# Batched fp32 matmul on one Trainium2 core: the first input load cut into eight transfers, and the last store moved into the hand-written section

## The chip, the cores and the metric

The kernel runs on 1 core of one Trainium2 chip. The metric is device time in microseconds (us), here the median of 3 runs: 262.35 us before the change, with single runs from 262.20 to 262.47 us.

## The reference

```python
def setup_inputs():
    batch, m, k, n = 16, 512, 768, 1024
    return {
        "x": np.random.randn(batch, k, m).astype(np.float32),
        "y": np.random.randn(batch, k, n).astype(np.float32),
    }

def reference(x: np.ndarray, y: np.ndarray) -> np.ndarray:
    return np.einsum('bkm,bkn->bmn', x, y).astype(np.float32)
```

Sixteen independent products: for each batch the 768x512 x, transposed, times the 768x1024 y. The contraction index k leads both inputs, so x needs no transpose on the chip. Per batch 1.57 MB of x and 3.15 MB of y are read and 2.10 MB of output are written, all fp32.

## The kernel before

**Layout.** k is split as 128 partitions by 6 (`ko`), so that one partition of x holds 12 KB that lie together in memory (6 x 512 floats), one partition of y 24 KB, and one partition of the output 16 KB (4 rows of 1024 floats). A load or store of one batch is one DMA instruction over all 128 partitions.

**Buffers.** x and y land in fp32 in two buffers each (`xs`, `ys`, by the batch's parity). VectorE casts them to bf16 (`xb`, `yb`, two slots each; lines 124 and 128). TensorE multiplies: 48 matmuls with 512 columns per batch, in two groups of 24 that fill the two halves of PSUM (line 150, in a hardware loop over the batches). ScalarE copies each half to an fp32 output buffer (line 166); there are five of those (`ob`, `NO = 5`). SyncE (SP) issues all DMAs, loads and stores alike, in one order on one queue.

**Order of the queue.** The whole kernel is written by hand inside one section (`tile_critical`, lines 45 and 46), in which the programmer places all semaphore waits. SP's part is the loop at line 102: for batch b it issues x (line 106), y (line 109) and, from b = 4 on (`LAG`), the store of batch b - 4 (lines 93 to 100). From b = 2 on, x waits until VectorE has cast the x of two batches before, and y likewise. After the loop come the stores of batches 12, 13 and 14 (line 112). GpSimd (line 131) passes VectorE's progress on to TensorE.

**Two shapes of load.** `wide_dma` (line 69) issues the first transfer of each kind, x and y, as an ordinary DMA (line 73). Each later one is a copy of that instruction with another access pattern: four x partitions, or two y partitions, are read as one row of 48 KB.

**Semaphores of the loads.** Each transfer adds 16 to the semaphore of its buffer (`sx[i]`, `sy[i]`) when it is complete. VectorE waits for 16 times the number of transfers into that buffer so far (line 123).

**The end.** The last store, of batch 15, is not in the section. At lines 174 and 175 SP waits until the stores of batches 11, 12 and 13 have landed; at line 176 the section is closed, which makes all engines meet; and line 181 issues the store of batch 15 outside of it, so that the Tile framework sets the waits around it, and waits for it to land before the program ends (line 207, the end of the launch).

Of the kernel before, what the change touches and what calls it, by code (L numbers as in the profile page):

```python
# [1 line left out]

_os.environ.setdefault("NEURON_RT_ULTRASERVER_MODE", "4")

# [2 lines left out]

# [5 lines left out]


@with_exitstack
def kernel(
    ctx: ExitStack,
    tc: tile.TileContext,
    x: bass.AP,
    y: bass.AP,  # L20
    out: bass.AP,
):
    nc = tc.nc
    P = 128
    FP32 = mybir.dt.float32
    BF16 = mybir.dt.bfloat16

    B, K, M = x.shape
    _, _, N = y.shape
    KT = K // P  # L30
    MT = M // P
    NF = 512
    NT = N // NF

    x_v = x.rearrange("b (p ko) m -> b p ko m", ko=KT)
    y_v = y.rearrange("b (p ko) n -> b p ko n", ko=KT)
    o_v = out.rearrange("b (p mo) n -> b p mo n", mo=MT)

    LAG = 4
    NO = 5
    KH = KT // 2

    section = ExitStack()
    section.enter_context(tc.tile_critical())
    ec = ctx.enter_context
    xs = [ec(nc.sbuf_tensor(f"xs{i}", [P, KT, M], FP32)) for i in range(2)]
    ys = [ec(nc.sbuf_tensor(f"ys{i}", [P, KT, N], FP32)) for i in range(2)]
    xb = ec(nc.sbuf_tensor("xb", [P, 2, KT, M], BF16))  # L50
    yb = ec(nc.sbuf_tensor("yb", [P, 2, KT, N], BF16))
    ob = [ec(nc.sbuf_tensor(f"ob{i}", [P, MT, N], FP32)) for i in range(NO)]

    HB = MT // 2
    ps = [ec(nc.psum_tensor(f"ps{i}", [P, HB, NT, NF], FP32)) for i in range(2)]
    sx = [ec(nc.semaphore(f"sx{i}")) for i in range(2)]
    sy = [ec(nc.semaphore(f"sy{i}")) for i in range(2)]
    so = [ec(nc.semaphore(f"so{i}")) for i in range(NO)]
    cast = ec(nc.semaphore("cast"))
    ready = ec(nc.semaphore("ready"))  # L60
    room = ec(nc.semaphore("room"))
    groups = ec(nc.semaphore("groups"))
    idle = ec(nc.semaphore("idle"))
    outs = ec(nc.semaphore("outs"))


    made = {}

    def wide_dma(key, dst, src, dram_rows, load):


        if key not in made:
            made[key] = nc.sync.dma_start(dst, src)
            return made[key]
        pat = mybir.BassSymbolicTensorAccessPattern
        widen = lambda a: a.rearrange("(q r) k m -> q (r k m)", r=dram_rows)
        plain = lambda a: a.rearrange("p k m -> p (k m)")
        s, d = (widen(src), plain(dst)) if load else (plain(src), widen(dst))
        return nc.sync.add_instruction(_copy.replace(
            made[key].ins, name=nc.get_next_instruction_name(),  # L80
            ins=(pat(ap=s.ap, dtype=s.dtype, bass_ap=s, is_dma=False),),
            outs=(pat(ap=d.ap, dtype=d.dtype, bass_ap=d, is_dma=False),),
            sync_info=None, ant_dge_precooked=False))


    def parts(b):
        return 2 if b in (15,) else 1


    nx = [sum(1 + parts(a) for a in range(b)) + 1 for b in range(B)]  # L90


    def store(b):


        if b < B - 2:
            nc.sync.wait_ge(groups, 2 * (b + 2))
        else:
            nc.sync.wait_ge(outs, b - (B - 3))
        nc.sync.dma_start(o_v[b], ob[b % NO][:]).then_inc(so[b % NO], 16)  # L100

    for b in range(B):
        i = b % 2
        if b >= 2:
            nc.sync.wait_ge(cast, nx[b - 2])
        wide_dma("x", xs[i][:], x_v[b], 4, True).then_inc(sx[i], 16)
        if b >= 2:
            nc.sync.wait_ge(cast, nx[b - 2] + parts(b - 2))
        wide_dma("y", ys[i][:], y_v[b], 2, True).then_inc(sy[i], 16)
        if b >= LAG:  # L110
            store(b - LAG)
    for b in range(B - LAG, B - 1):
        store(b)


    for _ in range(60):
        nc.vector.sem_inc(idle, 1)
    for b in range(B):
        i = b % 2
        n = 16 * (b // 2 + 1)  # L120
        if b >= 2:
            nc.vector.wait_ge(groups, 2 * (b - 1))
        nc.vector.wait_ge(sx[i], n)
        nc.vector.tensor_copy(xb[:, i], xs[i][:]).then_inc(cast, 1)  # L124
        nc.vector.wait_ge(sy[i], n)
        for h in range(parts(b)):
            ks = slice(h * KT // parts(b), (h + 1) * KT // parts(b))
            nc.vector.tensor_copy(yb[:, i, ks], ys[i][:, ks]).then_inc(cast, 1)  # L128


    for b in range(B):
        nc.gpsimd.wait_ge(cast, nx[b]).then_inc(ready, 1)
        for h in range(parts(b)):
            nc.gpsimd.wait_ge(cast, nx[b] + h + 1).then_inc(ready, 2 // parts(b))


    x_w = xb[:].rearrange("p s k (j mo) -> p s k mo j", mo=MT)
    pe = OrderedEngineSet([nc.tensor.engine])
    with nc.Fori(0, B // 2, engines=pe):
        with nc.Fori(0, 2, engines=pe) as s:  # L140
            nc.tensor.wait_ge(ready, 2).then_inc(ready, -2)
            for mo in range(MT):
                g, m = divmod(mo, HB)
                if m == 0:
                    nc.tensor.wait_ge(room, 1).then_inc(room, -1)  # L145
                for kt in range(KT):
                    if mo == 0 and kt == KH:
                        nc.tensor.wait_ge(ready, 1).then_inc(ready, -1)
                    for nt in range(NT):
                        mm = nc.tensor.matmul(  # L150
                            ps[g][:, m, nt], x_w[:, bass.ds(s, 1), kt, mo],
                            yb[:, bass.ds(s, 1), kt, nt * NF:(nt + 1) * NF],
                            start=(kt == 0), stop=(kt == KT - 1))
                if m == HB - 1:
                    mm.then_inc(groups, 1)


    nc.scalar.nop().then_inc(room, 2)
    for _ in range(60):
        nc.scalar.sem_inc(idle, 1)  # L160
    for b in range(B):
        if b >= NO:
            nc.scalar.wait_ge(so[b % NO], 16 * (b // NO))
        for g in range(2):
            nc.scalar.wait_ge(groups, 2 * b + g + 1)
            cp = nc.scalar.copy(ob[b % NO][:, g * HB:(g + 1) * HB].rearrange("p m (t f) -> p m t f", f=NF),  # L166
                                ps[g][:])
            if b < B - 1:
                cp.then_inc(room, 1)
        if b == B - 2:  # L170
            nc.scalar.drain().then_inc(outs, 1)
    cp.then_inc(outs, 1)

    for b in range(B - LAG - 1, B - 2):
        nc.sync.wait_ge(so[b % NO], 16 * (b // NO + 1))
    section.close()

    nc.sync.dma_start(o_v[B - 1], ob[(B - 1) % NO][:])


# [1 line left out]
_INS = ['x', 'y']  # L185
_OUTS = [((16, 512, 1024), 'float32')]


# [23 lines left out]
```

## Time and profile before

| what | us |
|---|---|
| median of 3 runs | 262.35 |
| the profiled execution, its own time | 262.47 |
| its span, first to last instruction | 260.7 |
| around the span | 1.8 |
| PE busy (matmul) | 186.1 |
| VectorE busy | 82.0 |
| ScalarE busy | 61.1 |
| share of 16 DMA engines' span, queue q1 | 98.1% |

PE is TensorE's matmul row, DVE is VectorE, ACT is ScalarE, SPq is SP's instruction stream. A line number such as L150 is a line of the kernel. "DMA share" is the mean busy share of the 16 DMA engines; a packet is counted in the stretch in which it starts, with its whole duration, so that a short stretch can show more than 1. The granted TensorE clock is given as a share of full speed. "Waits" lists who waited for whom; the chain is the work that ended last, followed back. All times in the views count from the start of the span.

### The profile page before, as it was taken

How to read it: one execution, taken by the hardware profiler on the slowest of the kernel's cores; microseconds unless marked ns; L12 is line 12 of the kernel's file. 1: busy time of each engine (PE TensorE's matmuls, PEld its weight loads, DVE VectorE, ACT ScalarE, POOL GpSimd, SP SyncE). 2: the span in 40 equal slices, each digit the busy share in tenths (PEclk: the TensorE clock that was granted, in tenths of full speed). 3: DMA queues.
4: the chain of work that ended last, by engine and by line, in shares of the span. 5: the costliest groups of instructions: out<-in, count | busy, mean ns of one | idle time of the engine just before them, and what ended most of it. 6: DMA issues, size and time to landing. Idle time of an engine off the chain costs nothing. (4 is left out here: it accounts for less than half of the span.)

```text
span 260.7 us, 2506 instructions
## 1 busy us (share of the span) xinstructions
PE 186.1 (71%) x768; PEld 89.8 (34%) x768; DVE 82.0 (31%) x33; ACT 61.1 (23%) x33; POOL 0.2 (0%) x4
## 2 busy tenths in 40 slices
PE   0009999998937949479596894969959197696910
PEld 0004555554512515124242351434425043253500
DVE  0261644525222252312524115252142522225000
ACT  1000442243220222202214022040322205022220
POOL 0000000000000000000000000000000000000000
PEclk9999999999995999959889797797999889799985
DMA  7998999999899899989999989999998999999994
GB/s 260 432 494 385 468 385 468 392 392 488 385 410 493 370 450 475 427 385 405 483 400 437 465 367 453 410 483 402 410 485 382 445 468 417 410 410 430 427 410 181
DMA packets 4514, 109.07 MB, mean 418 GB/s; under 512 B 768, under 2 KB 768, under 8 KB 768
## 3 DMA queue, kind: packets, MB, share of 16 engines
q1 hardware_dynamic: 4512, 109.05, 98.1%
q14 instruction: 2, 0.02, 0.0%
HBM read 75.50 MB, written 33.55 MB: 418 GB/s over the span
## 5 line engine op out<-in xcount | busy, mean ns | idle before, releaser
L150 PE MATMUL ps<-yb,xb 128*128 x768 | 186.1, 407 | 62.7 <-PEq L145 60.7
L150 PEld LDWEIGHTS ps<-yb,xb 128*128 x768 | 89.8, 117 | 158.5 <-issue 92.2
L166 ACT COPY ob<-ps 128x2048 f32<-128x2048 f32 x32 | 59.8, 1870 | 184.2 <-PE ps L150 184.2
L128 DVE CAST yb<-ys 128x6144 bf16<-128x6144 f32 (+1 forms) x17 | 53.8, 3171 | 87.7 <-DMA ys<-in_y_dram 87.7
L124 DVE CAST xb<-xs 128x3072 bf16<-128x3072 f32 x16 | 28.2, 1760 | 69.4 <-DMA xs<-in_x_dram 65.3
L166 ACT ACT_TABLE_LOAD x1 | 1.3, 1283 | 5.3 <-issue 5.3
L196 POOL MEMSET const-bfloat16-1.0<- 128x1 bf16 x1 | 0.1, 102 | 0.0
L196 POOL MEMSET const-uint8-127<- 128x1 uint8 x1 | 0.1, 102 | 0.0
L196 POOL MEMSET const-float32-1.0<- 128x1 f32 x1 | 0.1, 99 | 0.0
L196 POOL MEMSET const-float32-0.0<- 128x1 f32 x1 | 0.1, 98 | 0.2 <-issue 0.2
## 6 DMA issues: line engine op xcount, KB each, us to landing
ys<-in_y_dram SPq DMA_DIRECT2D x16, 3072.0 KB, 28.2
out_dram<-ob SPq DMA_DIRECT2D x16, 2048.0 KB, 32.6
xs<-in_x_dram SPq DMA_DIRECT2D x16, 1536.0 KB, 29.7
```

The source lines that it names most:

```text
L124: nc.vector.tensor_copy(xb[:, i], xs[i][:]).then_inc(cast, 1)
L128: nc.vector.tensor_copy(yb[:, i, ks], ys[i][:, ks]).then_inc(cast, 1)
L150: mm = nc.tensor.matmul(ps[g][:, m, nt], x_w[:, bass.ds(s, 1), kt, mo], yb[:, bass.ds(s, 1), kt, nt * NF:(nt + 1) * NF], start=(kt == 0), ...
L166: cp = nc.scalar.copy(ob[b % NO][:, g * HB:(g + 1) * HB].rearrange("p m (t f) -> p m t f", f=NF), ps[g][:])
L196: nc = _bacc.Bacc("TRN2", target_bir_lowering=False, num_devices=1)
```

## The change

The first x (batch 0) is issued as eight DMA instructions ahead of the loop. Transfer c takes the 16 partitions c, c + 8, c + 16 and so on. All eight add 16 to `sx[0]`, so that VectorE's waits on that semaphore are raised by 7 x 16 = 112. `wide_dma("x")` is called from b = 1 on, so that the x of batch 1 is now the first of its kind, issued as an ordinary DMA.

At the end the section is no longer closed by hand. The store of batch 15 is issued by SP within the section like the others, behind a wait for ScalarE's last copy; then SP waits for all five store semaphores, that of batch 15's store first; then the section ends, and with it the kernel.

```diff
-    section = ExitStack()
-    section.enter_context(tc.tile_critical())
+    ctx.enter_context(tc.tile_critical())
...
+    x_first = x_v[0].rearrange("(a c) k m -> a c k m", c=8)
+    for c in range(8):
+        nc.sync.dma_start(xs[0][c::8], x_first[:, c]).then_inc(sx[0], 16)
     for b in range(B):
         i = b % 2
         if b >= 2:
             nc.sync.wait_ge(cast, nx[b - 2])
-        wide_dma("x", xs[i][:], x_v[b], 4, True).then_inc(sx[i], 16)
+        if b > 0:
+            wide_dma("x", xs[i][:], x_v[b], 4, True).then_inc(sx[i], 16)
...
-    for b in range(B - LAG, B - 1):
+    for b in range(B - LAG, B):
         store(b)
...
-        nc.vector.wait_ge(sx[i], n)
+        nc.vector.wait_ge(sx[i], n + (112 if i == 0 else 0))
...
-    for b in range(B - LAG - 1, B - 2):
-        nc.sync.wait_ge(so[b % NO], 16 * (b // NO + 1))
-    section.close()
-    nc.sync.dma_start(o_v[B - 1], ob[(B - 1) % NO][:])
+    for i in range(NO):
+        nc.sync.wait_ge(so[i], 16 * len(range(i, B, NO)))
```

## The prediction

> **What bounds the kernel now.** I read the page's DMA rows first: queue, rate by slice, issues.
>
> ```profile
> PE 186.1 (71%) x768; PEld 89.8 (34%) x768; DVE 82.0 (31%) x33; ACT 61.1 (23%) x33; POOL 0.2 (0%) x4
> DMA  7998999999899899989999989999998999999994
> q1 hardware_dynamic: 4512, 109.05, 98.1%
> q14 instruction: 2, 0.02, 0.0%
> ys<-in_y_dram SPq DMA_DIRECT2D x16, 3072.0 KB, 28.2
> ```
>
> The DMA engines are busy 98.1% of the span; a y load waits 28.2 us from issue to landing, though its bytes need 3.15 MB / 430 GB/s = 7.3 us, so some 20 us of other transfers lie ahead of it. PE, at 71%, is not the bound. Two packets on q14 are instruction fetches.
>
> Then the ends of that stream: the timeline of SP, and the DMA by stretches (last column GB/s, the one before it the DMA share).
>
> ```profile
> 0.95 0.39 SPq L73 DMA_DIRECT2D xs<-in_x_dram  x1
> 1.39 0.42 SPq L73 DMA_DIRECT2D ys<-in_y_dram  x1
> 1.86 0.54 SPq L73 DMA_DIRECT2D xs<-in_x_dram  x1
> 2.44 0.60 SPq L73 DMA_DIRECT2D ys<-in_y_dram  x1
> ...
> 250.88 0.33 SPq L181 DMA_DIRECT2D out_dram<-ob  x1
> ```
>
> ```profile
> 0.95:1.95 1.00, 0.00 (x0) 0.00 (x0) 0.00 (x0) 0.00 (x0) 0.00 (x0) 1.00 0.00 0
> 1.95:2.50 0.55, 0.00 (x0) 0.00 (x0) 0.00 (x0) 0.00 (x0) 0.00 (x0) 1.00 1.74 268
> ```
>
> ```profile
> 252.00:256.50 4.50, 0.00 (x0) 0.00 (x0) 0.00 (x0) 0.00 (x0) 0.00 (x0) 0.50 1.00 426
> 256.50:257.50 1.00, 0.00 (x0) 0.00 (x0) 0.00 (x0) 0.00 (x0) 0.00 (x0) 0.50 0.16 66
> 257.50:258.50 1.00, 0.00 (x0) 0.00 (x0) 0.00 (x0) 0.00 (x0) 0.00 (x0) 0.50 0.12 49
> 258.50:259.00 0.50, 0.00 (x0) 0.00 (x0) 0.00 (x0) 0.00 (x0) 0.00 (x0) 0.50 0.08 33
> ```
>
> Issued at 0.95, the first bytes move at 1.98. At the end all engines run until 256.5, then two (0.12 of 16), then one (0.08 of 16). Following the trace's DMA records packet by packet (the next one starts as the last one ends) shows it: 12 engines end by 256.9, three at 257.5, 257.7 and 258.1, the slowest at 259.5. The slowest was never idle: its first packet starts at 2.07, its share of the first x ends at 6.54, it meets one q14 fetch (gap of 0.30 us at 11.4), and its first packet of the last store starts at 254.67, although that store was issued at 250.88. So the program's end is **the work of one DMA engine, from its first packet to its last**; ACT's last copy, which ends at 250.66 (the chain of waits), has some 3 us to spare on it.
>
> Last, who waits at the end, and what closing the section is made of (instructions of L46):
>
> ```profile
> SPq L175 <- DMA out_dram<-ob: 11.9, 1, 11.9
> SPq L207 <- DMA out_dram<-ob: 8.7, 1, 8.7
> ```
>
> ```profile
> L46 SPq EVENT_SEMAPHORE  x3: 17/28/28, 250.5 to 250.7; - x3
> L46 SPq COMPARE_BRANCH  x1: 33/33/33, 250.3 to 250.3; - x1
> L46 ACTq DRAIN  x1: 171/171/171, 250.5 to 250.5; - x1
> ```
>
> SP leaves L175 at 250.25; then branch, a signal to all engines, their drains, three semaphore steps, and at 250.88 the store. That is 0.63 us of meeting, passed while the slow engine still has 4 us of older work: it costs nothing today.
>
> **The change, part by part.**
>
> *The end.* Today: landing at 259.90, Tile's wait at 259.92, its next instruction at 259.97, end of span 260.69, so 0.77 us from wait to end. After: SP waits inside the section for the last store, and the 0.63 us of meeting come behind that wait, ahead of L207. The five waits go two to an instruction (L175's one instruction shows two semaphores, the third wait sits on the branch), so one more instruction, 250.25 to 250.32 = 0.07, runs after the landing. Tile's own wait goes, 259.92 to 259.97 = 0.05. Sum: 0.63 + 0.07 - 0.05 = **+0.65 us**, with nothing beside it: every other engine is done and waiting. Lower bound 0.45: ACT's drain took 0.17 because its last copy was still running, and if SP waited for it that part goes. Upper bound 0.80: each further wait has its own 0.07. That the store may be issued some 0.15 us sooner (238.02 for batch 14's against 237.97 for its copy, where batch 15's goes 0.22 after) is worth nothing, since the slow engine reaches it 4 us later.
>
> *The first x.* Bytes, rows and, if each transfer takes its 16 rows to 16 engines, the packets of each engine stay the same: 8 of 12 KB. What moves is the first packet, and what is added is seven issues and seven semaphore packets per engine. No row shows an issue of 16 rows. Its bounds: the last store, on idle engines, moved its first byte 0.83 after issue (250.88 to 251.71), the first x 1.03 after (0.95 to 1.98). As good as the store: gain 0.20. If the issue shrank to an eighth (0.39 to 0.05) and the 0.50 from the store's issue end to its first byte stayed: 0.55 after issue, gain 0.48. If nothing shrinks: 0. I take 0.20, the nearest row. The stagger between engines (1.98 to 3.10 on x, 0.1 us on the last store) is worth nothing to the bound: the slowest engine is among the ten that start by 2.08. Its first packet took 1.28 us against 0.46 of the others; should this cold part go too, it is 0.8 more (a rival below).
>
> *SP's queue.* Eight issues delay y of batch 0 and both loads of batch 1. At 0.44 each (0.95 to 1.39) y is issued at 4.5 and moves at 5.5; at 0.60 (the longest row) it is issued at 5.75 and moves at 6.8. The slow engine would finish x at about 6.35. So at 0.44 the eight packets hide the issues, with 0.8 to spare; at 0.60 the engine starves for 0.4. I take no loss. Nothing else waits in SP's queue until 9.05.
>
> *Small packets.* In the DMA records a semaphore packet adds 0.006 us from start to start, times 7 = 0.04. x of batch 1 as 8 packets of 12 KB (0.457 each) in place of 2 of 48 KB (1.811 each): 3.66 - 3.62 = 0.03. Sum +0.07, all on the bound. VectorE's raised wait adds no instruction.
>
> [...] In the row, the first x lands 6.3 us after issue (0.95 to 7.26) and y's packets start as x's end, so what is fixed in one transfer lies beside the data of another. [...] The row speaks against adding up fixed parts, so I don't.
>
> **Sum** against the profiled execution's own time: 262.47 + 0.65 - 0.20 + 0.07 = 262.99 us; that run lies 0.12 over the median of 262.35, so **262.9 us** is forecast (+0.2%). I hold 0.2%, 0.5 us, to be what a measurement here can tell from no change; the forecast is at that edge.
>
> **Rivals.**
>
> *Starved start.* If an issue costs over 0.55 us, the engines run out before y comes. For it: issues behind another took 0.54 and 0.60. Against: 16 rows are less work than 128. Price 0.1 to 0.6: 263.0 to 263.5.
>
> *The start gains more.* A gain near 0.48, or less cost at the end (0.45): 262.47 + 0.45 - 0.48 + 0.07 - 0.12 = 262.4, no change.
>
> *Faster: the slow engine's lag goes.* It ends 1.4 us behind the next and 2.6 us behind 12 others. Its delay began with the fetch at 11.4 and its cold packet, and grew where stores begin. If the new start shifts that fetch to another engine or shortens the cold packet by 0.8, up to 1.4 us go before the next engine sets the end, 2.6 if all end alike. It turns the sum below the time before once it is worth over 0.52. 0.8 gives 262.1, 2.6 gives 260.3. Against: nothing touches the fetch, and three runs within 0.27 us suggest a lag that comes back each time.
>
> *It does not do what it says:* the 16 rows spread over fewer engines. On 8 the first x takes twice 3.7 us, and the price is some 3.7 us: 266.5. [...] 2 in 100.
>
> **How the numbers follow.** Main case 0.62 (its own range, by the bounds 0.45 to 0.80 and 0 to 0.48: 262.4 to 263.2, its upper part over +0.2%): 0.36 slower, 0.26 same. Starved 0.13, slower. More gain at the start 0.10, same. Lag gone 0.13, faster. Fewer engines 0.02, slower. Slower 0.51, same 0.36, faster 0.13. The range from 262.1 to 263.5 takes in the bounds, the starved case and the small end of the faster one.
>
> **What would show it.** Right: in the changed profile, section instructions (L45 in its count of lines) between the last landing and L207, with about 1.4 us from landing to the end of the span in place of 0.8; first bytes between 1.5 and 1.9; the DMA share near 1 from 3.3 on without a hole at 6 to 7; one engine alone in the last 2 us. Wrong: a hole near 6.5 (starved), first bytes not earlier than 1.98, or a tail of the DMA shorter than 2 us with the rest unchanged (the lag is gone, and the main case falls).

## The result, and the profile after

The changed kernel takes **266.34 us** (median of 4 runs, 265.98 to 266.74) against 262.27 us before (4 runs, 261.99 to 262.47): a ratio of 1.0156, 95% interval 1.0138 to 1.0175, or +4.1 us (3.6 to 4.6). 262.9 was forecast, with a range from 262.1 to 263.5. The profiled execution took 266.49 us with a span of 264.6.

The page of the changed kernel, the rows that answer to those of before:

```profile
PE 187.7 (71%) x768; PEld 90.1 (34%) x768; DVE 82.0 (31%) x33; ACT 61.1 (23%) x33; POOL 0.2 (0%) x4
DMA  6999998999999899899999999899998999999993
q1 hardware_dynamic: 4720, 109.06, 97.7%
```

By busy time next to nothing has changed: the DMA engines still work 97.7% of the span. A packet is one piece that one DMA engine moves, here often the 12 KB of one partition. The number of packets grew by 208, as the diff says: 7 x 16 semaphore packets, and 96 data packets because the x of batch 1 is now moved in pieces of 12 KB.

VectorE's timeline tells where the time was lost. First before, then after:

```profile
7.26 1.76 DVE L124 CAST xb<-xs 128x3072 bf16<-128x3072 f32 x1 [7.26 <-DMA xs<-in_x_dram]
15.19 3.36 DVE L128 CAST yb<-ys 128x6144 bf16<-128x6144 f32 x1 [6.17 <-DMA ys<-in_y_dram]
```

```profile
11.02 1.76 DVE L128 CAST xb<-xs 128x3072 bf16<-128x3072 f32 x1 [11.02 <-DMA xs<-in_x_dram]
18.85 3.36 DVE L132 CAST yb<-ys 128x6144 bf16<-128x6144 f32 x1 [6.07 <-DMA ys<-in_y_dram]
```

The first x is there at 11.02 in place of 7.26, and the first y is as late, +3.66. The cast of the last y starts at 239.04 in place of 235.70, +3.34:

```profile
235.70 3.43 DVE L128 CAST yb<-ys 128x3072 bf16<-128x3072 f32 x2 [5.46 <-DMA ys<-in_y_dram]
```

```profile
239.04 3.43 DVE L132 CAST yb<-ys 128x3072 bf16<-128x3072 f32 x2 [5.59 <-DMA ys<-in_y_dram]
```

So nearly all is lost in the first 10 us and carried to the end. What happens there is in two stretches of equal length, 3.50 to 6.20, in which both kernels move nothing but the first x. Before and after (the last two columns are DMA share and GB/s):

```profile
3.50:6.20 2.70, 0.00 (x0) 0.00 (x0) 0.00 (x0) 0.86 (x1) 0.00 (x0) 1.00 1.01 432
```

```profile
3.50:6.20 2.70, 0.00 (x0) 0.00 (x0) 0.00 (x0) 0.86 (x1) 0.00 (x0) 1.00 1.04 219
```

All 16 engines are busy in both, and after the change they move half as much. In the DMA records a 12 KB packet of the first x takes 0.46 us before, and 0.94 us (the median) after: behind the first 16, 100 of 112 packets lie between 0.80 and 1.05.

SP's timeline and the first bytes, after:

```profile
0.95 5.04 SPq L104 DMA_DIRECT2D xs<-in_x_dram  x8
6.03 0.58 SPq L72 DMA_DIRECT2D ys<-in_y_dram  x1
```

```profile
0.95:1.95 1.00, 0.00 (x0) 0.00 (x0) 0.00 (x0) 0.00 (x0) 0.00 (x0) 1.00 0.00 0
1.95:2.50 0.55, 0.00 (x0) 0.00 (x0) 0.00 (x0) 0.00 (x0) 0.00 (x0) 1.00 0.48 134
```

Eight issues take 5.04 us, one every 0.63, where the single issue of 128 rows took 0.39. The first packet starts at 2.37 in place of 1.98: the smaller transfer starts later here, not earlier.

The end, by stretches and by the instructions that close the section:

```profile
254.00:259.50 5.50, 0.00 (x0) 0.00 (x0) 0.00 (x0) 0.00 (x0) 0.00 (x0) 0.81 1.00 426
259.50:260.50 1.00, 0.00 (x0) 0.00 (x0) 0.00 (x0) 0.00 (x0) 0.00 (x0) 0.50 0.16 66
260.50:261.50 1.00, 0.00 (x0) 0.00 (x0) 0.00 (x0) 0.00 (x0) 0.00 (x0) 0.50 0.11 49
```

```profile
L45 SPq EVENT_SEMAPHORE  x3: 17/28/28, 263.5 to 263.7; - x3
L45 SPq COMPARE_BRANCH  x1: 33/33/33, 263.3 to 263.3; - x1
L45 ACTq DRAIN  x1: 14/14/14, 263.5 to 263.5; - x1
```

The picture of before: all engines until 259.5, then two, then one. The last store lands at 263.33, the section is closed behind it, and the span ends at 264.57: 1.24 us from landing to end, 0.79 before.

### The profile page after: what moved, and what is told of

It reads as the page before. It is cut to its first block, busy times and chain, and to the rows that moved or that the text cites. A ratio compares the mean times of both kernels' runs of the same rounds, so it can differ in the third digit from the quotient of the medians.

```text
span 264.6 us, 2513 instructions
## 1 busy us (share of the span) xinstructions
PE 187.7 (71%) x768; PEld 90.1 (34%) x768; DVE 82.0 (31%) x33; ACT 61.1 (23%) x33; POOL 0.2 (0%) x4
## 3 DMA queue, kind: packets, MB, share of 16 engines
q1 hardware_dynamic: 4720, 109.06, 97.7%
```

## The experiments

The theory, formed on this: **(A) the side that is written decides: into some sets of partitions of SBUF, the memory on the chip, the engines write more slowly at one time than into others.** Its rivals: **(B)** rows that are read 96 KB apart collide in HBM, the memory that they are read from; **(C)** a transfer with one data packet for each engine is slow by itself; and that the end, not the start, makes the difference. Why one set should be slower than another was not shown by any run; what the runs test of A is which side of the transfer decides, and for which sets. The time of a packet, from the DMA records, is what tells A, B and C apart.

**e1: the end alone.** The diff's tail (store 15 inside the section, waits for all five semaphores), the first x as before:

```diff
...
-    for b in range(B - LAG, B - 1):
+    for b in range(B - LAG, B):
...
-    section.close()
-    nc.sync.dma_start(o_v[B - 1], ob[(B - 1) % NO][:])
+    for i in range(NO):
+        nc.sync.wait_ge(so[i], 16 * len(range(i, B, NO)))
```

> The end of the changed kernel alone (last store inside the section, waits for all five store semaphores behind it), with the first x as before in one transfer. All theories of the start say nothing here. By the prediction's sum for the end +0.65 us (0.45 to 0.80): a ratio of 1.0017 to 1.0031, and 1.3 to 1.5 us from the last landing to the end of the span in place of 0.8. In the changed kernel the landing of the last store is at 263.33 and the span ends at 264.57, 1.2 us later. If the end costs more than 1 us, the start is not the whole cause of the +4.1 us.

Measured: ratio 1.0015 (1.0004 to 1.0026), +0.39 us (0.1 to 0.7; the medians are 0.22 apart). In its trace 1.23 us pass from the last landing to the end of the span, 0.44 more than before. So the end costs about 0.4 us, and the start must carry the rest.

**e2: the eight transfers alone**, with the section closed by hand as before.

> The eight first transfers alone, with the end as before. In the changed kernel the cast of the first x starts at 11.02 in place of 7.26 (+3.8 us), and the cast of the last y at 239.04 in place of 235.70 (+3.3 us). If the start is carried to the end one for one, +3.3 to +3.8 us, ratio 1.0125 to 1.0145, with the packets of the first x again at about 0.94 us in place of 0.46. If the DMA stream catches up, or the +3.3 was of that one execution, less than +2.

Measured: ratio 1.0140 (1.0124 to 1.0157), +3.7 us; packets 0.936; cast of the first y +3.60, of the last y +3.25. The two parts alone, 3.7 and 0.4, add up to the 4.1 of the whole.

**e3: 16 neighbours** in place of every eighth:

```diff
-        nc.sync.dma_start(xs[0][c::8], x_first[:, c]).then_inc(sx[0], 16)
+        ps_ = slice(16 * c, 16 * (c + 1))
+        nc.sync.dma_start(xs[0][ps_], x_v[0][ps_]).then_inc(sx[0], 16)
```

> As e2, but transfer c takes the 16 neighbouring partitions from 16c on, on both sides, in place of every eighth. [...] Theory B, the reads from HBM at a stride of 96 KB collide: neighbouring rows don't, packets back at 0.46, the rest bound by 0.63 us for an issue, first x at about 8, kernel about +1 us. Theory C, a transfer with one data packet for each engine is slow by itself (the semaphore packet behind each packet): 0.94 again, kernel as e2.

Measured: ratio 1.0290 (1.0271 to 1.0310), +7.7 us, packets 1.58 (median), the first x at 15.61. The same stretch of e3:

```profile
3.50:6.20 2.70, 0.00 (x0) 0.00 (x0) 0.00 (x0) 0.56 (x1) 0.00 (x0) 1.00 1.07 137
```

B (0.46) and C (0.94) both fall in the form in which they were stated. A agrees as far as it goes: another set of partitions is written, and a packet takes 1.58 us, 3.4 times 0.46. A weaker B was left: that the place of the rows in HBM decides in some other way.

**e4: eight transfers of all 128 partitions**, 1.5 KB of each:

```diff
+    x_flat = x_v[0].rearrange("p k m -> p (k m)")
+    xs_flat = xs[0][:].rearrange("p k m -> p (k m)")
+    W = KT * M // 8
...
-        nc.sync.dma_start(xs[0][c::8], x_first[:, c]).then_inc(sx[0], 16)
+        cs = slice(W * c, W * (c + 1))
+        nc.sync.dma_start(xs_flat[:, cs], x_flat[:, cs]).then_inc(sx[0], 16)
```

> As e2, but each of the eight transfers takes all 128 partitions and one eighth of the columns (1.5 KB of a partition's 12 KB): eight issues and the same bytes each, all partitions at once. [...] The run measures what eight issues cost by themselves.

Measured: ratio 1.0029 (1.0018 to 1.0039), +0.75 us; packets 0.065 (median); issues of 0.43, one every 0.47:

```profile
3.50:6.20 2.70, 0.00 (x0) 0.00 (x0) 0.00 (x0) 0.86 (x1) 0.00 (x0) 1.00 0.88 246
```

As many issues with as many bytes each cost a fifth of e2 in the time of the kernel. It is not the price of the issues alone: eight packets of 1.5 KB take 0.52 us by the median and 0.65 by the mean, where one of 12 KB took 0.46. The first y was there at 17.17, +1.98, more than that; at the last y +0.86 was left. In this execution the slowest engine was 2.1 us behind the median engine at the last y, and 3.0 in the one of before; that hides 0.9 of it, and the median engine itself had made up 0.4 by batch 4, for no cause that was looked for.

**e5 and e6: the two sides swapped.** e5 reads every eighth row and writes 16 neighbours, e6 the other way round; if the written side decides, e5 goes as e3 and e6 as e2:

```diff
 e5
-        nc.sync.dma_start(xs[0][c::8], x_first[:, c]).then_inc(sx[0], 16)
+        nc.sync.dma_start(xs[0][16 * c:16 * (c + 1)], x_first[:, c]).then_inc(sx[0], 16)
 e6
-        nc.sync.dma_start(xs[0][c::8], x_first[:, c]).then_inc(sx[0], 16)
+        nc.sync.dma_start(xs[0][c::8], x_v[0][16 * c:16 * (c + 1)]).then_inc(sx[0], 16)
```

> As e2, but transfer c reads every eighth row of x (as the changed kernel) and writes 16 neighbouring partitions (as e3). The x of batch 0 is then in another order of k than its y, so batch 0 of the output isn't the reference's; amounts and times of work are the same. [...] Theory B in the form that e3 left (HBM side: the place of the 16 rows that are read at one time decides, 12 KB apart 1.58, 96 KB apart 0.94): packets as in e2, 0.94, kernel +3.7 us. An issue costs 0.59 with every eighth partition and 0.42 with neighbours; which side of the transfer makes that shows here too.

> The other way round: transfer c reads 16 neighbouring rows of x and writes every eighth partition; batch 0 of the output isn't the reference's. Theory A: packets 0.94, kernel as e2, +3.7 us. Theory B: packets 1.58, kernel as e3, +7.7 us.

Measured: e5 ratio 1.0306 (1.0289 to 1.0323), packets 1.52; e6 ratio 1.0127 (1.0111 to 1.0142), packets 0.90. First e5, then e6:

```profile
3.50:6.20 2.70, 0.00 (x0) 0.00 (x0) 0.00 (x0) 0.86 (x1) 0.00 (x0) 1.00 1.01 127
```

```profile
3.50:6.20 2.70, 0.00 (x0) 0.00 (x0) 0.00 (x0) 0.56 (x1) 0.00 (x0) 1.00 1.02 232
```

e5 is e3 (137 GB/s) and e6 is the changed kernel (219 GB/s): the rate follows the partitions that are **written**, whatever rows are read. B falls: with the same partitions written, the packets differ by 4% at most (1.52 and 1.58, 0.90 and 0.94), and the rows 96 KB apart are once the faster, once the slower. The length of an issue follows the written side too: 0.42 in e3 and e5, 0.59 in e2 and e6; and so does the first byte: 1.99 in e3 and e5, 2.37 and 2.36 in e2 and e6.

**e7: eight partitions, every fourth**, sixteen transfers:

```diff
-    x_first = x_v[0].rearrange("(a c) k m -> a c k m", c=8)
-    for c in range(8):
-        nc.sync.dma_start(xs[0][c::8], x_first[:, c]).then_inc(sx[0], 16)
+    x_first = x_v[0].rearrange("(q j c) k m -> q c j k m", j=8, c=4)
+    for q in range(4):
+        for c in range(4):
+            lo = 32 * q + c
+            nc.sync.dma_start(xs[0][lo:lo + 29:4], x_first[q, c]).then_inc(sx[0], 16)
...
```

> As e2, but sixteen transfers of 8 partitions each, every fourth one within a block of 32 (0, 4, ... 28, then 1, 5, ... 29 and so on). [...]

Measured, in one run: 269.4 us, +7.0, and the first x at 15.8. Of 112 packets behind the first 16, 46 took up to 0.50 us, 54 took 0.50 to 0.80, 12 more.

```profile
3.50:6.20 2.70, 0.00 (x0) 0.00 (x0) 0.00 (x0) 0.86 (x1) 0.00 (x0) 1.00 0.46 141
```

In its DMA records never more than eight packets of the first x are under way at once, so that the share of 0.46 is 0.92 of eight engines. Eleven issues take 7.54 us, one every 0.69, and a packet of the 112 takes 0.61 on the mean (0.55 the median): little is queued for each engine, and no run separates what that does to a packet. That 46 packets take no more than 0.50 us, with every fourth partition written, agrees with A; that the other 66 take longer is left unexplained, and the run is no clean proof.

**e8: the x of batch 1 in 12 KB packets, nothing else.** The edit is against the kernel of before.

```diff
+    nc.sync.dma_start(xs[0][:], x_v[0]).then_inc(sx[0], 16)
...
-        wide_dma("x", xs[i][:], x_v[b], 4, True).then_inc(sx[i], 16)
+        if b > 0:
+            wide_dma("x", xs[i][:], x_v[b], 4, True).then_inc(sx[i], 16)
```

> The first x in one transfer, but outside of the helper, so that the x of batch 1 is issued as an ordinary DMA (8 packets of 12 KB for each engine in place of 2 of 48 KB), the third part of the change by itself. The prediction's term: +0.03 us, nothing that can be measured (ratio within 0.998 to 1.002).

Measured: ratio 0.9996 (0.9984 to 1.0009). No difference, as expected.

**e9: every seventh partition**, seven transfers of 16, and the last 16 partitions in an eighth:

```diff
-    x_first = x_v[0].rearrange("(a c) k m -> a c k m", c=8)
-    for c in range(8):
-        nc.sync.dma_start(xs[0][c::8], x_first[:, c]).then_inc(sx[0], 16)
+    x_first = x_v[0][:112].rearrange("(a c) k m -> a c k m", c=7)
+    for c in range(7):
+        nc.sync.dma_start(xs[0][c:c + 106:7], x_first[:, c]).then_inc(sx[0], 16)
+    nc.sync.dma_start(xs[0][112:], x_v[0][112:]).then_inc(sx[0], 16)
```

> As e2, but the first seven transfers take every seventh partition (c, c + 7, ... c + 105) on both sides, the eighth takes the last 16. [...]

Measured: ratio 1.0095 (1.0078 to 1.0112), +2.5 us, the first x at 10.31.

```profile
3.50:6.20 2.70, 0.00 (x0) 0.00 (x0) 0.00 (x0) 0.76 (x1) 0.00 (x0) 1.00 0.80 273
```

The rate is higher than with a step of 8 although the engines are busy only 0.80 of the time: with packets of 0.55 (median) they now wait for issues, which come every 0.63. Of the 96 packets between the first 16 and the last 16, 35 took up to 0.50 us, 54 took 0.50 to 0.80, 7 more. So a step over partitions is not slow by itself: the median is 0.55 us with a step of 7 and 0.94 with a step of 8, and which partitions make up the set decides, as A says.

## Why the prediction was wrong

**What failed** is one sentence of "The first x": "the packets of each engine stay the same: 8 of 12 KB". Their number and size did stay; their duration was carried over with them, 0.46 us from the row of before, and it measured 0.94. That row belongs to a transfer of all 128 partitions. A longer packet was thus priced at nothing. The seven packets behind an engine's first cost 7 x (0.94 - 0.46) = 3.4 us by the medians; by the means it is 3.0 (0.88 against 0.46), because the second packet of an engine still took 0.64 and the fifth and sixth 0.86 and 0.91 (medians over the 16 engines). The other terms at the start nearly cancel: first byte 0.39 later, first packet shorter (0.66 against 1.21, the medians of the first 16), first packets of y longer (1.3 against 0.91, while other engines still finish x). Sum 3.6, against 3.66 at the first y; with 3.0 in place of 3.4 it is 3.2, so that the close agreement is partly luck. That this term is by far the largest holds either way.

**The first byte.** A gain of 0.20 was taken, bounds 0 to 0.48. It was a loss of 0.39, outside of the bounds: with every eighth partition the first issue takes 0.62 us, not less than the 0.39 of 128 rows. "16 rows are less work than 128" was wrong for the issue. That makes 0.23 of the 0.39; the other 0.16 lies between the end of the issue and the first byte (0.80 in place of 0.64), and no run takes it apart. e5 and e6 show that the step on the written side makes the whole: first bytes at 1.99 and 2.36.

**The issues.** The bound of 0.60 for one issue was about right (0.63 from one to the next), but the starved start did not come: at 0.94 us for a packet the engines are slower than the issues. With packets of 0.46 us the pace of 0.63 would have cost, by an estimate from these rows, 2.37 + 7 x 0.63 + 0.46 = 7.24 for the end of the first x against 6.89 before, about 0.35 us. The long packets hid it.

**The end.** +0.65 was summed, bounds 0.45 to 0.80; 0.44 to 0.45 came, in both traces. The landing of store 15 releases the branch itself, the last of SP's waits (branch at 263.35 behind the landing at 263.33), so the extra wait instruction passes earlier; and ACT's drain took 0.014 us in place of 0.171, since no copy was running any more. That was the reason given for the lower bound. The direction and the place, time behind the landing that nothing hides, were right.

**The bound.** "The work of one DMA engine, from its first packet to its last" held: the tail of two engines and then one is there again, and what was lost at the start came out at the end, 3.66 at the first y, 3.43 at the last landing. What was lost between is of the size by which the lag of the slowest engine differs between executions (2.0 to 3.2 us behind the median engine at the last y, in the traces of these runs).

**The small packets** cost nothing measurable (e8), as forecast.

**The rivals.** The case of fewer engines had the price that came, 266.5, by coincidence and not by its mechanism: all 16 worked (share 1.04). "Lag gone" did not come. The check that was named for the start, a DMA share near 1 without a hole, was met by a kernel that moved half the bytes. The sign of being wrong, first bytes not earlier than 1.98, was met as well: 2.37.

**What stays open.** That the partitions written at one time set the time of a packet is shown (1.58 us in e3, 1.52 in e5, 0.90 in e6, 0.55 in e9). What in SBUF makes one set slower than another is not. In e3's records the 16 packets of one transfer start over 0.83 us and take 1.58, so that half of the time two transfers are under way; what one such transfer alone would take no run shows. That fixed parts are not to be added up, as the prediction held, e4 bears out: seven more times the 1.03 us from issue to first byte would be, by an estimate from the row of before, +7.2 us, and eight transfers cost +0.75.

## What to carry to other kernels

A packet's duration belongs to the set of partitions that all engines write at one time: 12 KB took 0.46 us in a transfer to all 128, 0.55 in transfers to 16 that lie seven apart, 0.94 to 16 that lie eight apart, 1.58 to 16 neighbours. Before a transfer is cut by partitions, measure the packets of such a piece, and if it must be cut, cut the columns (e4: +0.75 us). Read the DMA share together with the rate: a share of 1 at half the GB/s is a traffic jam, not a busy stream (1.04 at 219 here, 1.01 at 432 before). And when a section is closed behind the last landing in place of ahead of it, its closing steps are paid in full, 0.4 us here.

## What the runs showed of the hardware that was not expected

- An issue of 16 rows is hardly cheaper than one of 128. Behind another issue it takes 0.42 us for 16 neighbouring partitions (e3), 0.43 for all 128 (e4), and 0.59 where the written partitions lie 8 apart (e2). What is read doesn't matter (e5 reads every eighth row: 0.42).
- DMA engines whose packets take two or three times as long count as busy all that time: a share of 1.04 at 219 GB/s, 1.07 at 137, 1.01 at 432.
- Sixteen engines on neighbouring partitions 0 to 15, 16 to 31 and so on moved 127 to 137 GB/s (e5, e3), with packets 3.3 to 3.4 times as long as on all 128.
